# First FFN group freed by halves, weight tiles per phase, squares summed on VectorE

## The chip, the cores and the metric
The kernel runs as one program on one core of a Trainium2 chip. The metric is the device time of one launch in microseconds. Three runs of the kernel before took 2505.52, 2515.11 and 2516.34 us. The profile is one further execution of 2504.3 us.

## The reference
A stack of four layers on x of 512 tokens by 1024 features, in float32. Each layer is a mixer and a SwiGLU feed-forward network (FFN), both behind an RMSNorm and both added to x.

```
def rmsnorm(x, w):
    y = xf * lax.rsqrt(jnp.mean(xf * xf, axis=-1, keepdims=True) + EPS)
    return (y * w.astype(jnp.float32)).astype(x.dtype)
def swiglu(h, w_in, w_out):
    gu = h @ w_in
    gate, up = gu[..., :D_FF], gu[..., D_FF:]
    return (jax.nn.silu(gate) * up) @ w_out
...
    for i in range(DEPTH):                       # layers 0 and 1
        hn = rmsnorm(x, norm_mix_w[i])
        x = x + mlstm_mixer(hn, ...)             # or window_attn_mixer
        x = x + swiglu(rmsnorm(x, norm_ffn_w[i]), ffn_w_in[i], ffn_w_out[i])
    return rmsnorm(x, norm_final_w)              # then layers 2 and 3 and a last norm
```

D_FF is 2816. The mixers are, in order: mLSTM in both directions, attention in a window, a parallel layer (sparse attention with an indexer beside Mamba2), and a gated short convolution. The norm that ends layer 1 and the norm that opens layer 2 follow each other directly; the kernel does both in one pass, called the double norm here.

## The kernel before
x is kept transposed, as eight tiles xT[0..7] of 128 features by 512 tokens. Every float32 product is made of three fp32r matmuls: each operand is split into a part hi (rounded to fp32r) and a rest lo, and hi·hi, hi·lo and lo·hi are added in one PSUM bank (mm3, L206 to L208). For an activation the parts are xh and xl, for a weight whi and wlo.

Weights come in blocks of 512 KB into wraw (five buffers, SyncE's queue). ScalarE makes whi by a copy (L170), VectorE makes wlo by a subtraction (L165; in the parallel mixer GpSimd does most of them). Both have four buffers of 4 KB per partition, in one pool wp that lives for the whole program. TensorE's last matmul with a buffer frees it.

The norm (L255) needs the sum of squares of each token over all eight tiles. ScalarE squares a tile into sq (one buffer), GpSimd adds it to ssum (L271). Then TensorE sums ssum over the partitions (col_sums, L239), VectorE computes 1/sqrt in 128x4 steps (rsqrt_cols, L229 to L234), TensorE spreads the result over all partitions by four transposes (bcast_rows, L245), and ScalarE copies it to rb (L246). The matmuls don't wait for rb: they use x times the norm's weight, and the result is multiplied by rb.

An FFN works on groups of 256 hidden features. The first group (first(), L475) is done plainly while the norm finishes: 8 k-tiles for each of two gate and two up blocks, with banks "s", "o", "s", "o". Bank "o" is a single one in the FFN, so the second up block comes later, when the first has been read. The gate half goes through VectorE (times rb) and Silu on ScalarE. Every further group is done by seven products in place of eight (a Strassen scheme over two halves of k and two of the tokens): product() with 24 matmuls of 128x256 (L421 to L423), whose activation operands are parts of x (B11, B21, B22) or their combinations T1 to T4, made by combine() (L371 to L377: S, fu, thi, tlo), and whose weight operands are weights or sums of them (S, L400 on GpSimd, L405 on VectorE). ahead() keeps three products' weights in preparation. After the groups of a part, out_part multiplies by the down weights, and add_row adds the result to xT (L493, L494).

The order of the instructions on each engine is set by a scheduler, from the code's dependencies and its own costs, and is fixed when the program is built. TensorE, VectorE, ScalarE and GpSimd work in that order; a wait holds up all that stands behind it on its engine.

Of the kernel before, what the change touches and what calls it, by code (L numbers as in the profile page):

```python
# [16 lines left out]
P = 128  # L17
# [40 lines left out]
def tile_net(ctx: ExitStack, tc: tile.TileContext, d, out, layers=(0, 1, 2, 3)):  # L58
# [12 lines left out]
    wp = ctx.enter_context(tc.tile_pool(name="wp", bufs=4))  # L71
# [20 lines left out]
    hidden = [None, None]  # L92

# [10 lines left out]
    WB = 4  # L104
# [79 lines left out]
    def load_a(w, k0, nk, c0, n):  # L184

        res = [[] for _ in range(0, n, P)]
        for k in range(0, nk, 4):
            m = min(4, nk - k)
            raw = load_raw(w, k0 + k, c0)
            hi, lo = split(raw, m, n)  # L190
            for b in range(0, n, P):
                res[b // P] += [(hi[:, i, b:b + P], lo[:, i, b:b + P]) for i in range(m)]
        return res

    def load_b(w, k0, nk, c0, n):
# [3 lines left out]
        for k in range(0, nk, mk):  # L199
            raw = load_raw(w, k0 + k, c0)  # L200
            hi, lo = split(raw, mk, n)
            res += [(hi[:, i, :], lo[:, i, :]) for i in range(mk)]
# [33 lines left out]
    def col_sums(ssum):  # L236
        ps = bank("t")
# [4 lines left out]
    def bcast_rows(rc, rb):  # L242
        ps = bank("t")
# [11 lines left out]
    def norm(wname, pre=None):  # L255
# [27 lines left out]
        for i, ssum in enumerate(sums):  # L283
            v = scr("nv", (P, NCH))
            V.tensor_scalar(v, col_sums(ssum), 1.0 / D, None if i else EPS, op0=ALU.mult,
                            **({} if i else dict(op1=ALU.add)))
            if i:
                V.tensor_tensor(v, v, rcs[0], op=ALU.mult)
                V.tensor_tensor(v, v, rcs[0], op=ALU.mult)
                V.tensor_scalar(v, v, EPS, None, op0=ALU.add)  # L290
            r = scr("nrc", (P, NCH), bufs=3)
            rsqrt_cols(r, v, NCH)
            rcs.append(r)
        if pre:
            V.tensor_tensor(rcs[1], rcs[1], rcs[0], op=ALU.mult)
            xs.rb1 = bcast_rows(rcs[0], row_tile())
        xs.rc = rcs[-1]
        xs.rb = bcast_rows(xs.rc, row_tile())
        return xs

    def group_a(xs, blocks, banks):
# [39 lines left out]
    def ffn(L, last=False, aside=None):  # L341
        wi, wd = f"in{L}", f"down{L}"
        xs = norm(f"ffn{L}")
        parts = [(0, 3), (3, 6), (6, 9), (9, 11)] if last else [(0, 4), (4, 8), (8, 11)]
        hid = {}
        rb2 = bass.AP(tensor=xs.rb.tensor, offset=xs.rb.offset, ap=[xs.rb.ap[0], [0, 2], [1, S]])
        HS = slice(0, S // 2), slice(S // 2, S)

        def gate(g):
            V.tensor_tensor(g, g, rb2, op=ALU.mult)  # L350
# [61 lines left out]
        def product(jj, s, ps, start):  # L412
            hi, lo = live.pop((jj, "w", s))
            x = quad(STEPS[s])
            for j in range(2):
                o = ps[:, HS[j]]
                for i in range(4):
                    c = slice(j * P, (j + 1) * P)
                    w = hi[:, i, c], lo[:, i, c]
# [179 lines left out]
    def mlstm():  # L599
# [12 lines left out]
        for k in (0, 4):  # L612
            hi = wp.tile([P, 4, P], F32R, tag="whi", name="ghi", bufs=WB)
# [1114 lines left out]
```

## Time and profile before

| | |
|---|---|
| runs | 2505.52, 2515.11, 2516.34 us |
| profiled execution | 2504.3 us, span 2502.2 us, mean granted clock 0.979 |
| TensorE (PE) busy | 2391.4 us, 96% |
| VectorE (DVE) busy | 1865.7 us, 75% |
| ScalarE (ACT) busy | 1139.0 us, 46% |
| GpSimd (POOL) busy | 526.8 us, 21% |
| squares added on GpSimd (L271) | 56 instructions, 92.5 us |
| where the phases lie | FFN of layer 0 opens near 271 us, that of layer 1 near 848, the double norm lies near 1223, the FFN of layer 2 opens near 1598, the short-conv mixer near 1940, its FFN near 2140 |

The span is the time from the first to the last instruction of the profile. The matmuls are pipelined, so a single one is shown longer than its share of the time; the distance from one start to the next says more. In the chain of waits that ended last TensorE has 83%, VectorE 9%, ScalarE 3%. The granted clock is a share of TensorE's full rate of 2.4 GHz; its other level is 1.2 GHz, shown as 0.50.

### The profile page before, as it was taken

What the parts mean: (1) busy time and instruction counts of PE and PEld (TensorE: products, weight loads), DVE (VectorE), ACT (ScalarE), POOL (GpSimd) and SP (SyncE); (2) the same over time, 40 slices, a digit from 0 to 9 for tenths busy, and PEclk for the clock granted to TensorE, in tenths of its full rate; (3) what the DMA queues carried; (4) which work ended last, traced back from release to release, by engine and by line L of the source; (5) the groups of instructions that cost most, each with busy time, mean ns of one, the idle gap of its engine ahead of it and who ended that gap; (6) DMA issues with size and microseconds to landing.
All of it is one profiled execution on the core that took longest, in us unless ns stands there. A gap on an engine that the chain in (4) does not pass through costs nothing.

```text
span 2502.2 us, 35838 instructions
## 1 busy us (share of the span) xinstructions
PE 2391.4 (96%) x14196; PEld 2087.2 (83%) x14196; DVE 1865.7 (75%) x2664; ACT 1139.0 (46%) x1739; POOL 526.8 (21%) x350
## 2 busy tenths in 40 slices
PE   8999899999899899999799988999999999999998
PEld 6887799998767799999567766798989777899997
DVE  5676887777776787777779968886867645868767
ACT  4444544444576553434444445453534323545334
POOL 3211201012362301011646235410000200200100
PEclk9999899999999899999899999999999999999999
DMA  4332232323311132323212133233323323223232
GB/s 146 119 102 60 67 123 85 118 81 115 97 47 34 59 118 85 119 85 99 76 61 63 47 110 93 61 102 92 117 92 103 99 84 95 85 92 122 83 110 76
DMA packets 73431, 226.58 MB, mean 91 GB/s; under 512 B 10336, under 2 KB 14576, under 8 KB 73264
## 3 DMA queue, kind: packets, MB, share of 16 engines
q1 hardware_dynamic: 68896, 220.00, 27.8%
q10 hardware_dynamic: 4320, 4.21, 0.6%
q8 instruction: 111, 1.82, 0.3%
q14 instruction: 56, 0.46, 0.1%
q0 software_dynamic: 48, 0.10, 0.0%
HBM read 219.45 MB, written 2.20 MB: 89 GB/s over the span
## 4 chain that ended last, share of the span: by engine, by line
PE 83%; DVE 9%; ACT 3%; DMA 2%; issue 2%; POOL 1%; ACTq 0%; SPq 0%; DVEq 0%; POOLq 0%
PE ps_g L206 6%; PE ps_g L207 6%; PE ps_g L208 6%; PE ps_g L423 5%; PE ps_g L421 5%; PE ps_g L422 5%; PE ps_s L206 3%; PE ps_s L207 3%; PE ps_s L208 3%; PE ps_t L423 3%; PE ps_t L422 3%; PE ps_t L421 3%; PE ps_t L206 3%; PE ps_t L207 3%; PE ps_t L208 3%
## 5 line engine op out<-in xcount | busy, mean ns | idle before, releaser
L170 ACT ACTIVATE whi<-wraw 128x1024 fp32r<-128x1024 f32 x358 | 372.9, 1044 | 544.3 <-PE ps_g L207 150.8
L165 DVE TENSOR_TENSOR wlo<-wraw,whi 128x1024 fp32r<-128x1024 f32 (+1 forms) x329 | 428.5, 1306 | 186.9 <-ACT whi L170 186.0
L400 POOL TENSOR_TENSOR S<-wraw 128x1024 f32<-128x1024 f32 x40 | 110.0, 2749 | 1012.9 <-DMA wraw<-in_in_dram 949.4
L170 ACT ACTIVATE whi<-S 128x1024 fp32r<-128x1024 f32 x160 | 169.5, 1060 | 244.5 <-PE ps_g L422 110.3
L206 PE MATMUL ps_g<-xh,whi 128*128 128x512 f32 (+1 forms) x632 | 258.2, 409 | 9.2 <-DVE ucv L1602 2.3
L165 DVE TENSOR_TENSOR wlo<-S,whi 128x1024 fp32r<-128x1024 f32 x160 | 210.9, 1319 | 64.4 <-ACT whi L170 64.2
L207 PE MATMUL ps_g<-xl,whi 128*128 128x512 f32 (+1 forms) x632 | 254.3, 403 | 0.2 <-DVE xl L279 0.2
L208 PE MATMUL ps_g<-xh,wlo 128*128 128x512 f32 (+1 forms) x632 | 253.7, 402 | 0.0
L423 PE MATMUL ps_g<-thi,wlo 128*128 128x256 f32 x640 | 181.4, 283 | 0.3 <-DVE wlo L165 0.3
L422 PE MATMUL ps_g<-tlo,whi 128*128 128x256 f32 x640 | 181.3, 283 | 0.0
L421 PE MATMUL ps_g<-thi,whi 128*128 128x256 f32 x640 | 181.3, 283 | 0.0
L206 PEld LDWEIGHTS ps_g<-xh,whi 128*128 128x128 f32 (+1 forms) x632 | 120.9, 191 | 39.5 <-issue 5.3
L208 PEld LDWEIGHTS ps_g<-xh,wlo 128*128 128x128 f32 (+1 forms) x632 | 121.2, 192 | 27.9 <-issue 2.6
L207 PEld LDWEIGHTS ps_g<-xl,whi 128*128 128x128 f32 (+1 forms) x632 | 121.2, 192 | 26.1 <-issue 2.0
L271 POOL TENSOR_TENSOR ssum<-ssum,sq 128x512 f32<-128x512 f32 x56 | 92.5, 1651 | 236.8 <-ACT sq L270 236.8
L423 PEld LDWEIGHTS ps_g<-thi,wlo 128*128 128x128 f32 x640 | 122.9, 192 | 0.5 <-DVE wlo L165 0.5
L421 PEld LDWEIGHTS ps_g<-thi,whi 128*128 128x128 f32 x640 | 123.0, 192 | 0.1
L422 PEld LDWEIGHTS ps_g<-tlo,whi 128*128 128x128 f32 x640 | 122.9, 192 | 0.1
L421 PE MATMUL ps_g<-xh,whi 128*128 128x256 f32 x320 | 94.1, 294 | 17.7 <-ACT whi L170 17.7
L207 PE MATMUL ps_s<-hlo,whi 128*128 128x512 f32 x264 | 102.9, 390 | 0.0
L208 PE MATMUL ps_s<-hhi,wlo 128*128 128x512 f32 x264 | 102.8, 389 | 0.0
L206 PE MATMUL ps_t<-hhi,whi 128*128 128x512 f32 x264 | 102.8, 389 | 0.0
(552 smaller groups left out, 7097.2 us busy)
## 6 DMA issues: line engine op xcount, KB each, us to landing
wraw<-in_in_dram SPq DMA_DIRECT2D x176, 512.0 KB, 3.6
wraw<-in_down_dram SPq DMA_DIRECT2D x82, 512.0 KB, 3.6
wraw<-in_par_in_dram SPq DMA_DIRECT2D x30, 512.0 KB, 3.5
wraw<-in_mlstm_in_dram SPq DMA_DIRECT2D x24, 512.0 KB, 3.8
wraw<-in_sc_in_dram SPq DMA_DIRECT2D x24, 512.0 KB, 3.5
wraw<-in_attn_in_dram SPq DMA_DIRECT2D x12, 512.0 KB, 4.1
wraw<-in_par_out_dram SPq DMA_DIRECT2D x12, 512.0 KB, 3.6
mb<-drs SPq DMA_DIRECT2D x16, 256.0 KB, 4.6
```

What stands on the lines that cost most here:

```text
L165: (V if e == "V" else G).tensor_tensor(lo, x, hi.bitcast(F32), op=ALU.subtract)
L170: A.activation(hi, raw, AF.Copy)
L206: T.matmul(o, lhsT=w[0], rhs=x[0], start=start, stop=False)
L207: T.matmul(o, lhsT=w[0], rhs=x[1], start=False, stop=False)
L208: T.matmul(o, lhsT=w[1], rhs=x[0], start=False, stop=stop)
L271: G.tensor_tensor(ssum, ssum, sq, op=ALU.add)
L400: G.tensor_tensor(live[jj, "S1"], live[jj, 2], live[jj, 3], op=ALU.add)
L421: T.matmul(o, lhsT=w[0], rhs=x[i][0], start=start and i == j == 0, stop=False, skip_group_check=True)
L422: T.matmul(o, lhsT=w[0], rhs=x[i][1], start=False, stop=False, skip_group_check=True)
L423: T.matmul(o, lhsT=w[1], rhs=x[i][0], start=False, stop=end, skip_group_check=True)
```

## The change
1. *Weight buffers per phase.* The pool wp goes. Each phase opens a pool of its own: in a mixer 8 buffers of 2 KB for whi and as many for wlo, in an FFN 4 of 4 KB. A tile of the new pool stands on memory of the phase before and waits for the last reader of just that memory (reuse_waits="tile"). split() cuts a block into pieces of the pool's width: in mixers load_a by blocks of 128 columns, load_b by two k-tiles, so whi and wlo are 128x512 there, and twice as many.
2. *The first FFN group.* Its weights are loaded as gate k 0 to 3, up k 0 to 3, gate k 4 to 7, up k 4 to 7, and k runs in its natural order (before: 0, 4, 1, 5, ..., with rows permuted on the host), so that a tile is used up halfway. The Strassen quadrants are k 0 to 3 and 4 to 7, and combine(i) pairs tiles i and i + 4.
3. *The FFN's norm inside the group.* col_sums and the rsqrt are written between k = 3 and k = 4, the broadcast at k = 6, on bank "s"; the group's banks are "t", "o", "t", "o".
4. *Squares' sums on VectorE* (7 additions per norm, 14 in the double norm, 56 in all). In the double norm both rsqrt chains are written first, then the two broadcasts.

The diff, cut to its core:

```
-    wp = ctx.enter_context(tc.tile_pool(name="wp", bufs=4))
...
+    def weight_tile(tag, name, nk, n):
+        pool, bufs, _ = weight_pool
+        return pool.tile([P, nk, n], F32R, tag=tag, name=name, bufs=bufs)
+
     def split(raw, nk, n):
-        hi = wp.tile([P, nk, n], F32R, tag="whi", name="whi", bufs=WB)
-        lo = wp.tile([P, nk, n], F32R, tag="wlo", name="wlo", bufs=WB)
-        A.activation(hi, raw, AF.Copy)
-        sub(lo, raw, hi)
-        return hi, lo
+        res = []
+        st = max(1, min(nk, weight_pool[2] // n))
+        for k in range(0, nk, st):
+            hi, lo = weight_tile("whi", "whi", st, n), weight_tile("wlo", "wlo", st, n)
+            A.activation(hi, raw[:, k:k + st, :], AF.Copy)
+            sub(lo, raw[:, k:k + st, :], hi)
+            res += [(hi[:, i, :], lo[:, i, :]) for i in range(st)]
+        return res
...
-                G.tensor_tensor(ssum, ssum, sq, op=ALU.add)
+                V.tensor_tensor(ssum, ssum, sq, op=ALU.add)
...
-    def group_a(xs, blocks, banks):
+    def group_a(xs, blocks, banks, between={}):
...
+            if k in between:
+                between[k]()
...
-        xs = norm(f"ffn{L}")
+        xs = norm(f"ffn{L}", tag="s", later=True)
...
         def first():
-            order = [0, 4, 1, 5, 2, 6, 3, 7]
-            bg = [[b[k] for k in order] for b in load_a(wi, 0, KT, 0, 256)]
-            bu = [[b[k] for k in order] for b in load_a(wi, 0, KT, DFF, 256)]
-            pss = group_a(xs, [bg[0], bu[0], bg[1], bu[1]], ["s", "o", "s", "o"])
+            ws = [], [], [], []
+            for k in (0, 4):
+                for n, c in enumerate((0, DFF)):
+                    for hi, lo in split(load_raw(wi, k, c), 4, 256):
+                        for i in range(2):
+                            ws[n + 2 * i].append([t[:, i * P:(i + 1) * P] for t in (hi, lo)])
+            pss = group_a(xs, ws, ["t", "o", "t", "o"], {4: xs.sums, 6: xs.rows})
...
+    TILE = dict(reuse_waits="tile")
...
+            with wpool(f"wm{L}", 8, 512), tc.tile_pool(name=f"hm{L}", bufs=8) as hidden[0], \
+                    tc.tile_pool(name=f"mix{L}", bufs=2) as phase[0]:
                 mixers[L]()
...
+        with wpool(f"wf{L}", 4, 1024), tc.tile_pool(name=f"tf{L}", bufs=4, **TILE) as hidden[1], \
+                tc.tile_pool(name=f"hf{L}", bufs=4, **TILE) as hidden[0], \
+                tc.tile_pool(name=f"ff{L}", bufs=2, **TILE) as phase[0]:
             ffn(L, last=last, aside=rope_tables if before_window else None)
```

How the order moves, at three places. ScalarE at the opening of layer 0's FFN, before (xT_116 is xT[7], xT_115 is xT[6]; thi are the combinations' hi parts):

```order
150 L270 ACTIVATE sq<-xT_113 128x512
151 L270 ACTIVATE sq<-xT_114 128x512
152 L222 ACTIVATE thi<-fu 128x1024
153 L270 ACTIVATE sq<-xT_115 128x512
154 L222 ACTIVATE thi<-fu 128x1024
155 L270 ACTIVATE sq<-xT_116 128x512
156 L170 ACTIVATE whi<-wraw 128x1024 x2
157 L170 ACTIVATE whi<-S 128x1024
```

The same place after (xT_113 is xT[7], xT_112 is xT[6]):

```order
153 L289 ACTIVATE xh<-xT_112,cols 128x512
154 L394 ACTIVATE S<-xT_112,cols 128x512
155 L176 ACTIVATE whi<-wraw 128x1024 x4
156 L281 ACTIVATE sq<-xT_110 128x512
157 L289 ACTIVATE xh<-xT_113,cols 128x512
158 L232 ACTIVATE thi<-fu 128x1024
159 L394 ACTIVATE S<-xT_109,cols 128x512
160 L394 ACTIVATE S<-xT_113,cols 128x512
161 L232 ACTIVATE thi<-fu 128x1024
162 L281 ACTIVATE sq<-xT_111 128x512
163 L176 ACTIVATE whi<-wraw 128x1024
164 L281 ACTIVATE sq<-xT_112 128x512
```

Before, the group's four whi stood far ahead of this piece, among the mixer's, and the first products' whi (row 156) behind the last square. After, the group's four whi stand together in row 155, behind xT[6], and the first product's whi (row 163) stands ahead of the last squares.

ScalarE from layer 0's FFN to the window mixer, before (xT_112 to xT_116 are xT[3] to xT[7]):

```order
301 L278 ACTIVATE xh<-xT_112,cols 128x512
302 L170 ACTIVATE whi<-wraw 128x1024 x2
303 L278 ACTIVATE xh<-xT_113,cols 128x512
304 L270 ACTIVATE sq<-xT_112 128x512
305 L278 ACTIVATE xh<-xT_114,cols 128x512
306 L270 ACTIVATE sq<-xT_113 128x512
307 L270 ACTIVATE sq<-xT_114 128x512
308 L170 ACTIVATE whi<-wraw 128x1024
309 L278 ACTIVATE xh<-xT_115,cols 128x512
310 L170 ACTIVATE whi<-wraw 128x1024
```

And after:

```order
315 L289 ACTIVATE xh<-xT_111,cols 128x512
316 L281 ACTIVATE sq<-xT_111 128x512
317 L289 ACTIVATE xh<-xT_112,cols 128x512
318 L281 ACTIVATE sq<-xT_112 128x512
319 L176 ACTIVATE whi<-wraw 128x512 x8
320 L289 ACTIVATE xh<-xT_113,cols 128x512
```

The mixer's first four whi, which stood among the last tiles of x, have become eight of half the size that stand together behind xT[6].

TensorE at the end of the double norm, before (nrc are the norm's factors; L1115 transposes the indexer's key weights):

```order
6633 L207 MATMUL ps_g<-xl,whi 128x512
6634 L208 MATMUL ps_g<-xh,wlo 128x512
6635 L245 MATMUL ps_t<-ident,nrc 128x128 x8
6636 L1115 MATMUL ps_t<-ident,ikw 128x8 x4
6637 L206 MATMUL ps_g<-xh,whi 128x512
```

After, with the two pieces of the order that hold the broadcasts:

```order
6610 L218 MATMUL ps_s<-xh,wlo 128x512
6611 L255 MATMUL ps_t<-ident,nrc 128x128 x4
6612 L216 MATMUL ps_g<-xh,whi 128x512
```

```order
6634 L217 MATMUL ps_g<-xl,whi 128x512
6635 L218 MATMUL ps_g<-xh,wlo 128x512
6636 L255 MATMUL ps_t<-ident,nrc 128x128 x4
6637 L1140 MATMUL ps_t<-ident,ikw 128x8 x4
6638 L216 MATMUL ps_g<-xh,whi 128x512
```

The eight transposes that stood together are two sets of four now, with the 24 matmuls of rows 6612 to 6635 between them.

## Rows read from the trace of the kernel before
**Rows 1.** Busy time and share of the span of each engine, from the page
```profile
PE 2391.4 (96%) x14196; PEld 2087.2 (83%) x14196; DVE 1865.7 (75%) x2664; ACT 1139.0 (46%) x1739; POOL 526.8 (21%) x350
```
**Rows 2.** Timeline of PE: start us, us, instruction [idle before <-what ended it]
```profile
279.60 0.58 PE L421 MATMUL ps_g<-xh,whi 128*128 128x256 f32 x1 [8.11 <-ACT whi L170]
...
856.16 0.58 PE L421 MATMUL ps_g<-xh,whi 128*128 128x256 f32 x1 [8.12 <-ACT whi L170]
...
1225.06 0.62 PE L245 MATMUL ps_t<-ident,nrc 128*128 128x128 f32 x4 [1.96 <-DVE nrc L234]
1235.14 1.09 PE L245 MATMUL ps_t<-ident,nrc 128*128 128x128 f32 x4 [9.46 <-DVE nrc L295]
1238.45 0.56 PE L1115 MATMUL ps_t<-ident,ikw 8*128 8x8 f32 x4 [2.22 <-DVE ikw L1111]
...
1381.62 0.30 PE L1393 MATMUL ps_o<-pth,N 128*128 128x128 f32 x1 [2.57 <-DVE cy L1410]
...
1616.03 1.87 PE L239 MATMUL ps_t<-ones,ssum 128*128 128x1 f32 x8 [2.52 <-POOL ssum L271]
...
1644.68 0.50 PE L206 MATMUL ps_o<-xh,whi 128*128 128x512 f32 x1 [1.53 <-DVE fu L487]
...
1968.36 1.11 PE L245 MATMUL ps_t<-ident,nrc 128*128 128x128 f32 x4 [2.43 <-DVE nrc L234]
1971.61 0.79 PE L206 MATMUL ps_g<-xh,whi 128*128 128x512 f32 x1 [2.14 <-DVE ct L1601]
...
2161.20 0.65 PE L245 MATMUL ps_t<-ident,nrc 128*128 128x128 f32 x4 [0.53 <-DVE nrc L234]
```
**Rows 3.** Windows of PE: stretch, us, busy (instructions), granted clock, DMA share, GB/s
```profile
279.60:290.00 10.40, 10.40 (x56) 0.60 0.16 52
856.20:866.00 9.80, 9.80 (x63) 0.74 0.18 55
1235.10:1246.00 10.90, 8.64 (x29) 0.61 0.01 2
1616.00:1628.00 12.00, 10.31 (x52) 0.59 0.15 45
1968.40:1980.00 11.60, 9.46 (x29) 0.61 0.01 1
1382.00:1390.00 8.00, 7.91 (x29) 0.79 0.01 2
1640.00:1648.00 8.00, 5.00 (x26) 1.00 0.26 68
1598.00:1646.00 48.00, 39.28 (x225) 0.89 0.19 58
```
**Rows 4.** Timeline of ACT ahead of the first FFN's first product
```profile
277.97 0.63 ACT L270 ACTIVATE sq<-xT 128x512 f32<-128x512 f32 x1 [3.47 <-POOL ssum L271]
278.50 1.99 ACT L170 ACTIVATE whi<-wraw 128x1024 fp32r<-128x1024 f32 x2
```
**Rows 5.** Timelines: what one matmul, split or addition takes; from the page, the squares
```profile
1218.18 0.39 PE L206 MATMUL ps_g<-xh,whi 128*128 128x512 f32 x1
...
1222.71 0.39 PE L208 MATMUL ps_g<-xh,wlo 128*128 128x512 f32 x1
...
1937.79 0.63 ACT L170 ACTIVATE whi<-wraw 128x512 fp32r<-128x512 f32 x1 [0.35 <-PE ps_t L207]
...
1619.72 1.22 DVE L165 TENSOR_TENSOR wlo<-wraw,whi 128x1024 fp32r<-128x1024 f32 x1
...
1947.97 0.68 DVE L493 TENSOR_TENSOR fg<-ps_s,rb 128x512 f32<-128x512 f32 x1
...
L271 POOL TENSOR_TENSOR ssum<-ssum,sq 128x512 f32<-128x512 f32 x56 | 92.5, 1651 | 236.8 <-ACT sq L270 236.8
```
**Rows 6.** Timelines of DVE and POOL in the double norm
```profile
1235.03 1.19 DVE L1363 TENSOR_SCALAR nrc<-nrc 128x4 f32<-128x4 f32 x1
...
1226.40 9.80 POOL L1414 TENSOR_TENSOR xT<-xT,rb 128x512 f32<-128x512 f32 x8 [3.41 <-ACT rb L246]
```

More of the change, by code (lines that the diff above doesn't have):

```diff
@@ L1 @@
-from contextlib import ExitStack
+from contextlib import ExitStack, contextmanager
 import numpy as np
@@ L189, in load_a @@
             raw = load_raw(w, k0 + k, c0)
-            hi, lo = split(raw, m, n)
+            if weight_pool[2] >= m * n:
+                w4 = split(raw, m, n)
+                for b in range(0, n, P):
+                    res[b // P] += [(hi[:, b:b + P], lo[:, b:b + P]) for hi, lo in w4]
+                continue
             for b in range(0, n, P):
-                res[b // P] += [(hi[:, i, b:b + P], lo[:, i, b:b + P]) for i in range(m)]
+                res[b // P] += split(raw[:, :, b:b + P], m, P)
         return res
@@ L200, in load_b @@
             raw = load_raw(w, k0 + k, c0)
-            hi, lo = split(raw, mk, n)
-            res += [(hi[:, i, :], lo[:, i, :]) for i in range(mk)]
+            res += split(raw, mk, n)
         return res
@@ L234, in rsqrt_cols, with col_sums @@
             V.scalar_tensor_tensor(y, z, 1.5, y, op0=ALU.add, op1=ALU.mult)
-    def col_sums(ssum):
-        ps = bank("t")
+    def col_sums(ssum, tag="t"):
+        ps = bank(tag)
         for c in range(NCH):
@@ L240, in col_sums, with bcast_rows @@
         return ps[:, 0:NCH]
-    def bcast_rows(rc, rb):
-        ps = bank("t")
+    def bcast_rows(rc, rb, tag="t"):
+        ps = bank(tag)
         for c in range(NCH):
@@ L253, in row_tile, with norm @@
         return sp.tile([P, S], F32, tag="rb", name="rb", bufs=2)
-    def norm(wname, pre=None):
+    def norm(wname, pre=None, tag="t", later=False):
         xs = XS()
@@ L282, in norm, with scales, rows @@
         rcs = []
[L283 to L298, printed above, removed]
+        def scales():
+            for i, ssum in enumerate(sums):
+                v = scr("nv", (P, NCH))
+                V.tensor_scalar(v, col_sums(ssum, tag), 1.0 / D, None if i else EPS, op0=ALU.mult,
+                                **({} if i else dict(op1=ALU.add)))
+                if i:
+                    V.tensor_tensor(v, v, rcs[0], op=ALU.mult)
+                    V.tensor_tensor(v, v, rcs[0], op=ALU.mult)
+                    V.tensor_scalar(v, v, EPS, None, op0=ALU.add)
+                r = scr("nrc", (P, NCH), bufs=3)
+                rsqrt_cols(r, v, NCH)
+                rcs.append(r)
+            if pre:
+                V.tensor_tensor(rcs[1], rcs[1], rcs[0], op=ALU.mult)
+            xs.rc = rcs[-1]
+        def rows():
+            xs.rb = bcast_rows(xs.rc, row_tile(), tag)
+            if pre:
+                xs.rb1 = bcast_rows(rcs[0], row_tile(), tag)
+        xs.sums, xs.rows = scales, rows
+        if not later:
+            scales()
+            rows()
         return xs
-    def group_a(xs, blocks, banks):
+    def group_a(xs, blocks, banks, between={}):
         n = len(xs.t)
@@ L418, in product @@
                     c = slice(j * P, (j + 1) * P)
-                    w = hi[:, i, c], lo[:, i, c]
+                    w = [t[:, c] for t in ws[i]]
                     end = i == 3
@@ L612, in mlstm @@
         for k in (0, 4):
-            hi = wp.tile([P, 4, P], F32R, tag="whi", name="ghi", bufs=WB)
-            lo = wp.tile([P, 4, P], F32R, tag="wlo", name="glo", bufs=WB)
+            hi = weight_tile("whi", "ghi", 4, P)
+            lo = weight_tile("wlo", "glo", 4, P)
             G.memset(hi.bitcast(F32), 0.0)
@@ L1081, in parallel @@
             G.memset(raw[:, :, 72:96], 0.0)
-            hi, lo = split(raw[:, :, 0:112], 4, 112)
-            sm += [(hi[:, i, :], lo[:, i, :]) for i in range(4)]
+            sm += split(raw[:, :, 0:112], 4, 112)
         lay = ExitStack()
@@ L1617, in tile_net, with wpool @@
     rope = ExitStack()
+    TILE = dict(reuse_waits="tile")
+    @contextmanager
+    def wpool(name, bufs, width):
+        with tc.tile_pool(name=name, bufs=bufs, **TILE) as pool:
+            weight_pool[:] = pool, bufs, width
+            yield
     for n, L in enumerate(layers):
@@ L1625, in tile_net @@
         if L == 2:
[L1626 removed]
+            with wpool(f"wm{L}", 8, 512), tc.tile_pool(name=f"hm{L}", bufs=8) as hidden[0]:
                 parallel(n > 0)
         else:
[L1629 removed]
+            with wpool(f"wm{L}", 8, 512), tc.tile_pool(name=f"hm{L}", bufs=8) as hidden[0], \
+                    tc.tile_pool(name=f"mix{L}", bufs=2) as phase[0]:
                 mixers[L]()
```

18 lines of the change are left out of this document (6 added, 12 removed).

## The prediction
> **What bounds the kernel now.** I read five views in this order. The busy shares come first: TensorE is busy 96% of the span [rows 1], so there are some 111 us in which it stands still, and only these, and the stretches in which its clock is low, can be won back. The second view is TensorE's timeline, cut to the instructions that come after an idle stretch of 2 us or so [rows 2]. The reader is to see where they lie: each of the first two FFNs opens with a hole of 8 us that ends when ScalarE delivers a weight tile (L170); the double norm ahead of the parallel mixer has three holes (1.96, 9.46 and 2.22 us); the third FFN has several small ones; the short-conv mixer has two (2.43 and 2.14 us); the fourth FFN has almost none (0.53 us). The third view gives the granted clock behind such holes [rows 3]. Behind the first hole TensorE works 10.40 us at a mean of 0.60, so it loses 0.40 x 10.40 = 4.2 us more; behind the second 0.26 x 9.80 = 2.5 us. Not every hole does that: behind 2.57 us the loss is 0.21 x 7.91 = 1.7 us, and in 1640 to 1648, where two holes of about 1.5 us lie, the clock stays at 1.00. The fourth view is ScalarE ahead of the first hole [rows 4]: it waits 3.47 us for GpSimd's addition of squares before the last square, and only then turns the weights. The matmuls had ended at 279.60 - 8.11 = 271.49, and since all four weight buffers were theirs, nothing could be prepared earlier. The fifth view are the unit costs [rows 5] and what GpSimd does to VectorE [rows 6].
>
> **What the places cost now**, idle plus clock: first FFN 8.11 + 4.2 = 12.3; second 8.12 + 2.5 = 10.6; third 48 - 39.28 = 8.7 idle in the whole opening stretch, plus 0.41 x 10.31 = 4.2, together 12.9; fourth 0.53 in rows 2, I take 0.8 with what is below my cut. Four FFNs: 36.6. Double norm 13.64 + 0.39 x 8.64 = 17.0. Short-conv start 4.57 + 0.39 x 9.46 = 8.3. (All [rows 2, 3].)
>
> **The change part by part.** T is the end of the last matmul before a phase. A 128x512 matmul comes every (1222.71 - 1218.18) / 20 = 0.227 us; one of 128x256 I take at half, 0.113 (an estimate); a Strassen product has 24 of them, 2.7 us. Two whi of 4 KB take 1.99 us [rows 4], so 1.0 each; one of 2 KB 0.63; wlo of 4 KB 1.22; an addition of 128x512 on VectorE 0.68 [rows 5].
>
> (1) FFN openings. The group's first tile (gate k 0 to 3) is now used up halfway, so the first product's tile is turned while the group still runs, and the hole of 8 us goes. Three things are late next.
> First, the weights of the group itself. The pool is new per phase, so its tiles stand on memory that the mixer still reads: in the order, ScalarE's four whi come after xh and S of xT[6], and the last of them waits for T. The first whi ends near T + 0.5 (first FFN) or T + 1.0 (second, which waits for T itself); VectorE adds xT[7] (T + 0.8) and two 128x256 pieces before wlo, which ends near T + 2.7; TensorE has six matmuls (1.4 us) to do meanwhile. Idle: 2.7 - 1.4, about 1.4 us with latencies; third FFN 1.05 (no pieces in the way), fourth 0.7 (its first whi is early). Before, this cost nothing.
> Second, the third product. Until the second half of the "up" blocks is done (they share the one bank "o" and come after the fourth product), two of four buffers stay with the group. The third product's whi therefore waits for the end of the second product: 1.1 us to the first matmul, then wlo 1.22 of which two matmuls cover 0.2. That is 2.1 us idle in the first and second FFN, 3.0 in the third, where a subtraction of 1.2 us and two smaller things stand ahead of that wlo on VectorE, 1.6 in the fourth, where the broadcast covers 0.5.
> Third, the row broadcast. It now stands behind the third product, and the fourth product needs the bank that the gate is read from. Behind the transposes queue ScalarE's whi (1.1 us after the product), rb (0.63), and VectorE's wlo (to 2.3) and the multiplication (0.68): 3.0 in all, less some 0.5 of the transposes (four take up to 0.62 [rows 2]), 2.55 us. The fourth FFN has its broadcast earlier and pays nothing here.
> The clock: pairs of about 1.5 us left it alone, 2.57 us cost 1.7 [rows 2, 3]; the third hole is of that size, so I take 1.7 for each of the first three FFNs, with 0 and 4.2 as ends.
> After: 1.4 + 2.1 + 2.55 + 1.7 = 7.8 twice; 1.05 + 3.0 + 2.55 + 1.7 = 8.3; 2.3. Together 26.2 against 36.6: **-10.4**. Ends: the second and third hole could be covered by nothing that the trace shows, so they could also be 1.5 us each longer (4 x 3 = +12), or vanish where ScalarE and VectorE run ahead (about -14).
>
> (2) Double norm. Before, the two broadcasts stand together, and the chain for the second runs while GpSimd scales xT for 9.80 us; each of VectorE's tiny 128x4 steps then takes 1.19 us [rows 6], whereas the whole chain of twelve in the short-conv norm costs TensorE 2.43 us [rows 2]. After, both chains are computed first, 24 matmuls (5.4 us) stand between the broadcasts, and GpSimd's scaling follows the second. What is left is the wait for ikw behind the second broadcast, 2.2 us as now [rows 2], plus 0.8 for clock: 17.0 - 3.0 = **-14.0**. Ends: weight halves on GpSimd still run beside the chain, so up to 5 us may come back; at best 17 - 2.2.
>
> (3) Short-conv start. 24 matmuls now stand between sums and broadcast, so the 2.43 us go; the wait for ct stays (2.14), alone and with no clock behind it: 8.3 - 2.2 = **-6.1**. Ends 0 and -8.
>
> (4) FFN to mixer, three times. Before, the first mixer weights were turned while the FFN still multiplied; now eight whi of 2 KB stand together and the first waits for the FFN's last matmuls, with VectorE's wlo behind an add and a square's sum: 0.55 + 0.1 + 0.5, near 1.2 us each: **+3.6**. Ends 1.5 and 9 (with clock).
>
> (5) Squares on VectorE: 56 additions of 0.68 = 38 us there [rows 5], none on TensorE's path: the column sums stand 15 matmuls into the first product, at T + 20, and I count the last addition at T + 14 to 16. Cover gone, they would cost up to these 38. In the bargain xl and the small steps meet GpSimd less. Nothing.
> (6) 2 KB tiles in mixers: 2 x 0.63 for 1.0 on ScalarE, 0.25 more per tile; ScalarE is busy 46% [rows 1]. Nothing, with 0 to +4, since the parallel mixer is crowded on VectorE. The start of the program is split finer: nothing, 0 to -3.
>
> Sum: -10.4 - 14.0 - 6.1 + 3.6 = -26.9. The profiled execution took 2504.3 us (span 2502.2 and 2.1 around it), so it would take 2477. The median of the runs shown, 2515.11, lies 10.8 above; the forecast in its terms is **2488 us**.
>
> **Rivals.** (a) *The clock takes it back* (other side). The new holes lie close together: 1.4, then 2.1 and 2.55 within 6 us. If at each FFN both places drop the clock as the 8 us hole does, that is 8.4 us instead of 1.7 (0 in the fourth): +28.5, hence 2516; with a drop at the three mixer starts too, 3 x 4.2 more, 2529. It decides from the second place on in all four FFNs. For it: the third FFN's opening ran at 0.59 for 12 us with holes of 2.5 and less. Against: 1640 to 1648 at 1.00 [rows 3].
> The Trainium skill, "TensorE: Matmul & The Clock Gate", section "A second HAM failure mode: psum-queue depth-cycling", says that short idle stretches between groups of matmuls, if they come often enough, make the clock swing between its two levels; by that rule this rival's 2516 would come, and of this trace 1616 to 1628 agrees with it and 1640 to 1648 does not.
> (b) *VectorE becomes the bound.* It is busy 75% [rows 1], and gets 38 us of sums. If half of that stands on the path, 2488 + 19 = 2507. For: in the third FFN's opening and in the norms little of its time is free. Against: the sums are needed late.
> The Trainium skill, "SBUF — State Buffer", section "Who interferes with whom", says that a VectorE instruction with two SBUF inputs and a GpSimd instruction that reads SBUF lock each other out; the moved additions are of that kind, and the 1.19 us steps beside GpSimd's 9.80 agree in direction [rows 6].
> (c) *Better*: the second and third hole hardly appear and the clock holds: 26.2 falls to about 12, 2474.
> (d) *The halves free nothing*: the group's last buffers gate the products as before; the FFNs stay at 36.6, 2488 + 10.4 = 2498.
>
> **How the numbers follow.** Forecast 0.50, (c) 0.18, (d) 0.08, (b) 0.12, (a) 0.12. Half a percent, about what a measurement here tells from no change, is 12.6 us: 2502.5 and 2527.7. Faster: 0.50 + 0.18 + 0.08 = 0.76; same: 0.10 of (b) and 0.05 of (a); slower: 0.07 of (a) and 0.02 of (b), 0.09. Range 2466 to 2512: below (c) by the ends of (2) and (4), above (b), short of (a).
>
> **What would show it.** Right: no hole of 8 us at the FFN starts; in each FFN opening one of about 1.4 that ends with VectorE's wlo, one near 2.1 ended by ScalarE's whi and VectorE's wlo two products later, and one near 2.5 ended by VectorE's reading of the gate; the double norm with a single hole near 2.2; holes near 1.2 at the mixer starts. Wrong: a clock near 0.6 behind these, sums that end later than the first product, VectorE's busy share over 85% in the openings, or a hole of several us in the parallel mixer that is not there now.

## The result and the profile after

The changed kernel took 2479.14 us (median of four runs, 2478.45 to 2483.95), the kernel before 2512.11 beside it (four runs, 2505.52 to 2516.34). The ratio is 0.9875, with a 95% interval of 0.9848 to 0.9903. The forecast of 2488 us was made against a median of 2515.11; in its own terms, 2477.4 over 2504.3, it is 0.9893 and lies inside. The total was right; most of where it came from was not, and that the errors nearly cancelled was luck. The profiled execution of after took 2479.76 us (span 2478.1). That of before (2504.3) lies 8 us below the median of its runs, so the two profiles show some 24.5 of the 33 us.

The page of after, which answers to [rows 1]: GpSimd lost its 56 additions, VectorE's total hardly rose, TensorE's busy time fell by 3 us.

```profile
PE 2388.4 (96%) x14196; PEld 2088.1 (84%) x14196; DVE 1866.2 (75%) x2826; ACT 1160.3 (47%) x1869; POOL 437.2 (18%) x318
```

TensorE's timeline of after, which answers to [rows 2] (start, us, instruction, idle before and what ended it): the first FFN's opening, a piece of the second's, the double norm, the short-conv start.

```profile
248.38 0.50 PE L216 MATMUL ps_t<-xh,whi 128*128 128x512 f32 x1 [0.86 <-ACT whi L176]
...
251.00 0.73 PE L218 MATMUL ps_t<-xh,wlo 128*128 128x512 f32 x2 [0.95 <-DVE wlo L164]
...
271.50 0.38 PE L446 MATMUL ps_s<-xh,wlo 128*128 128x256 f32 x1 [1.27 <-DVE wlo L164]
...
275.42 0.39 PE L444 MATMUL ps_g<-thi,whi 128*128 128x256 f32 x1 [1.03 <-ACT whi L176]
...
276.68 0.39 PE L446 MATMUL ps_g<-thi,wlo 128*128 128x256 f32 x1 [0.76 <-DVE wlo L164]
...
283.72 0.58 PE L444 MATMUL ps_t<-thi,whi 128*128 128x256 f32 x1 [3.71 <-DVE fg L510]
...
859.02 0.39 PE L446 MATMUL ps_g<-thi,wlo 128*128 128x256 f32 x1 [0.76 <-DVE wlo L164]
859.24 0.28 PE L444 MATMUL ps_g<-thi,whi 128*128 128x256 f32 x1
859.36 0.37 PE L445 MATMUL ps_g<-tlo,whi 128*128 128x256 f32 x1
859.53 0.41 PE L446 MATMUL ps_g<-thi,wlo 128*128 128x256 f32 x1
859.74 0.41 PE L444 MATMUL ps_g<-thi,whi 128*128 128x256 f32 x1
...
1225.56 0.65 PE L255 MATMUL ps_t<-ident,nrc 128*128 128x128 f32 x4 [1.92 <-DVE nrc L308]
...
1228.39 0.56 PE L1140 MATMUL ps_t<-ident,ikw 8*128 8x8 f32 x4 [2.18 <-DVE ikw L1136]
...
1957.41 0.50 PE L216 MATMUL ps_g<-xh,whi 128*128 128x512 f32 x1 [2.14 <-DVE ct L1626]
```

The hole of 8 us is gone; in its place stand six, together 8.58 us, so TensorE is idle no less than before. The last ends when VectorE has read the gate. In the second FFN, in the middle of a product, the distance between starts goes from 0.12 to 0.21 us at 859.53: the clock fell half a microsecond behind a hole of 0.76, ahead of the gate's hole. At the double norm the 9.46 of [rows 2] is gone.

Windows of TensorE in after, answering to [rows 3] (stretch, us, busy and instructions, granted clock, DMA share, GB/s); the last is the window mixer without its ends:

```profile
274.00:282.00 8.00, 4.23 (x32) 1.00 0.43 156
282.00:290.00 8.00, 6.28 (x28) 0.57 0.00 0
857.00:865.00 8.00, 5.32 (x28) 0.79 0.35 131
865.00:873.00 8.00, 6.72 (x34) 0.79 0.00 0
1600.00:1608.00 8.00, 3.65 (x25) 0.93 0.26 74
1608.00:1616.00 8.00, 5.85 (x27) 0.64 0.33 124
1616.00:1624.00 8.00, 8.00 (x41) 0.79 0.00 0
1228.00:1236.00 8.00, 7.61 (x23) 0.57 0.05 19
1957.00:1965.00 8.00, 7.59 (x26) 0.79 0.21 68
605.00:829.00 224.00, 209.76 (x969) 0.95 0.19 59
```

ScalarE at the first FFN, answering to [rows 4]. The group's weight tiles start right behind xh and S of xT[6]. The first product's whi (255.85) is made while the group runs, ahead of the last squares. These still wait for additions, now VectorE's (1.62 and 2.65 us), but no weight tile stands right behind them.

```profile
246.04 0.73 ACT L289 ACTIVATE xh<-xT,cols 128x512 fp32r<-128x512 f32 x1 [1.05 <-DVE xT L348]
246.67 0.71 ACT L394 ACTIVATE S<-xT,cols 128x512 f32<-128x512 f32 x1
247.28 2.94 ACT L176 ACTIVATE whi<-wraw 128x1024 fp32r<-128x1024 f32 x3
...
255.85 1.05 ACT L176 ACTIVATE whi<-wraw 128x1024 fp32r<-128x1024 f32 x1
258.52 0.63 ACT L281 ACTIVATE sq<-xT 128x512 f32<-128x512 f32 x1 [1.62 <-DVE ssum L282]
261.80 0.63 ACT L281 ACTIVATE sq<-xT 128x512 f32<-128x512 f32 x1 [2.65 <-DVE ssum L282]
```

**Time by phase**, in us, from the end of the last matmul of the phase before to that of its own, read off TensorE's timeline in one profile of each kernel. The variants below are in it, to be read with the experiments. "par" is the parallel mixer with the double norm, "FFNs" the sum of the four.

| kernel | mLSTM | FFN 0 | window | FFN 1 | par | FFN 2 | conv | FFN 3 | FFNs |
|---|---|---|---|---|---|---|---|---|---|
| before | 255.0 | 356.7 | 219.9 | 355.3 | 408.3 | 358.9 | 189.2 | 349.5 | 1420.4 |
| after | 247.4 | 357.1 | 225.2 | 356.3 | 389.5 | 360.0 | 181.3 | 351.7 | 1425.1 |
| before, sums on VectorE | 254.5 | 354.0 | 223.0 | 354.0 | 406.4 | 359.2 | 188.7 | 349.0 | 1416.1 |
| before, order of double norm | 255.2 | 358.8 | 222.9 | 355.9 | 405.6 | 361.2 | 188.2 | 349.5 | 1425.3 |
| before, both of these | 253.6 | 353.7 | 226.0 | 354.2 | 392.8 | 360.8 | 188.0 | 349.0 | 1417.7 |
| after, sums on GpSimd | 247.5 | 354.7 | 228.1 | 353.0 | 399.0 | 362.0 | 182.1 | 352.3 | 1422.0 |
| after, one pool | 254.7 | 353.8 | 222.2 | 356.0 | 387.5 | 360.7 | 188.4 | 348.3 | 1418.7 |
| after, no halves | 245.3 | 354.4 | 224.3 | 353.2 | 391.5 | 359.8 | 181.5 | 352.1 | 1419.4 |
| after, norm ahead | 245.5 | 349.0 | 223.8 | 350.5 | 404.4 | 357.0 | 179.9 | 349.6 | 1406.0 |
| after, other banks | 247.0 | 346.4 | 223.0 | 346.4 | 393.6 | 348.8 | 181.4 | 348.6 | 1390.2 |

So the FFNs, for which most of the change was written, gave nothing (+4.7 together). The gain is the parallel mixer (-18.8), the short-conv mixer (-7.9) and the mLSTM mixer (-7.6). A phase whose code two kernels have in common differs by up to some 4 us between their profiles where the order of the instructions is nearly the same, and by 15 in the parallel mixer of "after, norm ahead", which the scheduler ordered in another way (experiment 10). So differences of 4 us in the table carry nothing, and there is one profile of each kernel.

### The profile page after: what moved, and what is told of

The parts are those of the page before. It is cut to its first block, busy times and chain, and to the rows that moved or that the text cites. A ratio compares the mean times of both kernels' runs of the same rounds, so it can differ in the third digit from the quotient of the medians.

```text
span 2478.1 us, 36192 instructions
## 1 busy us (share of the span) xinstructions
PE 2388.4 (96%) x14196; PEld 2088.1 (84%) x14196; DVE 1866.2 (75%) x2826; ACT 1160.3 (47%) x1869; POOL 437.2 (18%) x318
## 4 chain that ended last, share of the span: by engine, by line
PE 82%; DVE 10%; DMA 2%; ACT 2%; issue 2%; POOL 1%; ACTq 0%; SPq 0%; DVEq 0%; POOLq 0%
PE ps_g L216 6%; PE ps_g L218 6%; PE ps_g L217 6%; PE ps_g L446 5%; PE ps_g L445 5%; PE ps_g L444 5%; PE ps_s L216 4%; PE ps_s L218 3%; PE ps_s L217 3%; PE ps_t L444 3%; PE ps_t L445 3%; PE ps_t L446 3%; PE ps_t L217 3%; PE ps_t L216 3%; PE ps_t L218 3%; DVE wlo L164 2%
## 5 line engine op out<-in xcount | busy, mean ns | idle before, releaser
L176 ACT ACTIVATE whi<-wraw 128x512 fp32r<-128x512 f32 (+1 forms) x488 | 394.7, 819 | 614.0 <-PE ps_g L217 195.8
L164 DVE TENSOR_TENSOR wlo<-wraw,whi 128x512 fp32r<-128x512 f32 (+1 forms) x428 | 441.1, 1040 | 173.2 <-ACT whi L176 164.3
L423 POOL TENSOR_TENSOR S<-wraw 128x1024 f32<-128x1024 f32 x40 | 117.0, 2924 | 1161.7 <-DMA wraw<-in_in_dram 995.1
L164 POOL TENSOR_TENSOR wlo<-wraw,whi 128x512 fp32r<-128x512 f32 (+1 forms) x60 | 79.6, 1336 | 142.0 <-ACT whi L176 96.2
L217 PE MATMUL ps_t<-hlo,whi 128*128 128x512 f32 x264 | 102.7, 389 | 0.0
```

The source lines that it names most:

```text
L164: (V if e == "V" else G).tensor_tensor(lo, x, hi.bitcast(F32), op=ALU.subtract)
L176: A.activation(hi, raw[:, k:k + st, :], AF.Copy)
L217: T.matmul(o, lhsT=w[0], rhs=x[1], start=False, stop=False)
L423: G.tensor_tensor(live[jj, "S1"], live[jj, 2], live[jj, 3], op=ALU.add)
```

## The experiments

Ratios are to the kernel before, run on the same chip, with 95% intervals.

**1. Squares added on VectorE, in the kernel before.**
```
-                G.tensor_tensor(ssum, ssum, sq, op=ALU.add)
+                V.tensor_tensor(ssum, ssum, sq, op=ALU.add)
```


> The kernel before, with the 56 additions of squares (L271) moved from GpSimd to VectorE and nothing else. Theory (the 8 us holes before came from ScalarE waiting for GpSimd's additions, not from weight tiles that were held too long): the first product's whi follows the end of the group by about 1 us, the holes at the first two FFN starts fall from 8.1 to about 2 us without loss of clock, the third FFN loses its 2.5 us hole; about 25 us faster than before, near 2487. Rival (the halves of the group free the tiles, the additions were beside the path): the holes stay near 8 us, at most 5 us faster, 2507 or more.

Measured 2500.3 us, 0.9969 (0.9957 to 0.9982), between the two. TensorE's timeline at the first FFN and the double norm:

```profile
271.69 0.38 PE L421 MATMUL ps_g<-xh,whi 128*128 128x256 f32 x1 [0.66 <-ACT whi L170]
...
1233.07 1.09 PE L245 MATMUL ps_t<-ident,nrc 128*128 128x128 f32 x4 [11.61 <-DVE nrc L295]
```

With the tiles held as before and only the additions moved, the 8.11 us fell to 0.66 here, and 1.91, 0.27 and later 1.47 and 0.99 came: FFN 0 is 2.7 us shorter, not 8. So most of the big hole was cover for smaller lateness. The big hole itself came from ScalarE. ScalarE's timeline here:

```profile
270.59 1.04 ACT L170 ACTIVATE whi<-wraw 128x1024 fp32r<-128x1024 f32 x1
...
272.49 0.61 ACT L270 ACTIVATE sq<-xT 128x512 f32<-128x512 f32 x1
```

and the addition that the last square waits for in [rows 4], from GpSimd's timeline of before:

```profile
273.29 4.64 POOL L271 TENSOR_TENSOR ssum<-ssum,sq 128x512 f32<-128x512 f32 x1 [4.05 <-ACT sq L270]
```

That addition took 4.64 us, against a mean of 1.65. With the additions on VectorE the last square starts at 272.49 in place of 277.97, 5.5 us earlier. And the scheduler's order moved with the edit: the first product's whi now stands ahead of that square and no longer behind it, so it starts at 270.59 in place of 278.50, 7.9 us earlier. What the order would give alone, no run shows.

**2. Squares back on GpSimd, in the changed kernel** (the same line the other way).

> The changed kernel with the 56 additions of squares back on GpSimd and nothing else. Theory (the sums are read only 15 matmuls into the first product, so who makes them matters little once first() and the pools are changed, but sq has one buffer and ScalarE waits for its reader): holes of 1 to 4 us come back where ScalarE waits for GpSimd ahead of a whi, 5 to 12 us slower than the changed kernel, 2484 to 2491. Rival (the move to VectorE is the main gain): 20 us or more slower, 2500.

Measured 2489.0 us, 0.9908 (0.9880 to 0.9937), some 8 us above after by the ratios, whose intervals overlap. Nearly all of it lies in the parallel mixer (399.0 against 389.5). The 8 us holes did not come back in the FFNs, though the additions are GpSimd's again: the first product's whi is made at 260.14 us, ahead of the squares that wait for GpSimd (1.31 and 3.00 us). Holes of 2.4 to 4.1 us came at five phases' starts.

**3. No halves: the changed kernel with k interleaved in the first group**, so that every tile is read to the end.
```
-        for k in range(n):
+        for i, k in enumerate((0, 4, 1, 5, 2, 6, 3, 7) if between else range(n)):
```


> The changed kernel, but the first group takes k in the order 0, 4, 1, 5, 2, 6, 3, 7, so that all four weight tiles are read to the end (norm inside, pools and sums as changed). Theory (halves only hide the first product's conversion): the first product starts 1 us late and waits 1.2 us for wlo, some 2 us more idle in each FFN, about 8 us slower than the changed kernel, near 2487. Rival (halves are what took the 8 us holes away): holes near 8 us again with the clock behind them, 25 to 35 us slower, near 2510.

Measured 2474.28 us, 0.9868 (0.9853 to 0.9882): not slower than after. The holes of the first opening are 0.86, 0.94, 2.45, 0.59 and 0.76, together 5.60. Neither expectation came. Freeing the tiles by halves is worth nothing that can be measured here.

**4. One pool of 4 KB buffers for the whole program, in the changed kernel.**
```
-        with tc.tile_pool(name=name, bufs=bufs, **TILE) as pool:
-            weight_pool[:] = pool, bufs, width
-            yield
+        weight_pool[:] = wp, 4, 1024
+        yield
```


> The changed kernel with one weight pool of 4 buffers of 4 KB for the whole program again (and so 4 KB tiles in the mixers). Theory (a new pool per phase makes the first weights wait for the last matmul of the phase before): the holes at the phase starts go (0.9 and 0.9, 0.9 and 0.9, 1.5 and 1.4 at three FFN starts; 0.5 to 1.8 at three mixer starts), about 10 us less, near 2469. Rival (the 2 KB tiles bring more inside the mixers than the starts cost): the holes of 0.8 us in the short-conv mixer and those at the program's start come back, 0 to 8 us slower, 2479 to 2487.

Measured 2484.71 us, 0.9914 (0.9896 to 0.9931). In the table the mLSTM and short-conv mixers go back to their times before (254.7 and 188.4), and the FFNs lose the cost of a fresh pool (1418.7). The short-conv start:

```profile
1949.13 0.65 PE L256 MATMUL ps_t<-ident,nrc 128*128 128x128 f32 x4 [2.43 <-DVE nrc L245]
1951.92 0.79 PE L217 MATMUL ps_g<-xh,whi 128*128 128x512 f32 x1 [2.14 <-DVE ct L1627]
```

Both holes of [rows 2] stand there to the hundredth, and five more of 0.78 to 0.88 us behind them (4.1 us) as in the kernel before. What shortened these mixers are the 2 KB tiles and not the pool per phase: in experiment 7, with one pool of 2 KB tiles, they take 246.3 and 179.9 us.

**5. Other banks for the first group, in the changed kernel.** Bank "s" has three buffers in an FFN, "t" and "g" two, "o" one.
```
-        xs = norm(f"ffn{L}", tag="s", later=True)
+        xs = norm(f"ffn{L}", tag="g", later=True)
...
-            pss = group_a(xs, ws, ["t", "o", "t", "o"], {4: xs.sums, 6: xs.rows})
+            pss = group_a(xs, ws, ["s", "o", "s", "t"], {4: xs.sums, 6: xs.rows})
```


> The changed kernel with other PSUM banks in the first group: gate blocks on s, s, up blocks on o and t, the norm's sums and broadcast on g. No bank that the next four products write is then held by the gate, and the second up block doesn't wait for the first to be read, so all four weight tiles are used up within the group. Theory (the holes at the third and fourth product come from the two tiles held by the up blocks and from the gate's bank): holes of 1.0, 0.8 and 2.5 to 3.7 us go in the first three FFNs, with the clock behind them; 15 to 20 us less than the changed kernel, near 2461. Rival (VectorE and ScalarE are simply behind in the opening, whichever bank it is): the holes move to other products, 0 to 5 us less, 2474 to 2479.

Measured 2446.58 us, 0.9759 (0.9745 to 0.9774): 29 us below after by the ratios, more than was expected. TensorE's windows over the first three openings:

```profile
247.00:290.00 43.00, 41.91 (x259) 1.00 0.30 98
816.00:860.00 44.00, 42.67 (x266) 1.00 0.29 96
1556.00:1600.00 44.00, 42.26 (x250) 0.96 0.31 96
```

About 1.1 to 1.7 us idle in each, the clock at 1.00, 1.00 and 0.96. All four blocks have a bank, so the group's 96 matmuls run before the first product where 72 did, and no product waits for the gate: the FFNs are 34.9 us shorter than in after.

**6. The same banks without halves** (the edits of 3 and 5 together).

> The kernel with the other banks (e8), but with k in the order 0, 4, 1, 5, 2, 6, 3, 7 in the first group, so that no weight tile is used up before the group ends. Theory (with the banks out of the way the halves do their work: they let two products' weights be turned inside the group): a hole of 1.0 plus 1.4 us at each FFN's first product and about 1 at the second, with no clock behind it; 8 to 14 us slower than e8, 2455 to 2460. Rival (the halves are worth nothing here either, as with the banks of the changed kernel): within 3 us of e8.

Measured 2445.67 us, 0.9742 (0.9718 to 0.9765), the same as 5. Halves are worth nothing here either. These two are the best versions run.

**7. The same banks, with one pool of eight 2 KB buffers.**
```
+        weight_pool[:] = wp, 8, 512
```


> The kernel with the other banks (e8) and, in place of a pool per phase, one pool of 8 buffers of 2 KB for the whole program, so that weights are split in pieces of 128x512 in the FFNs too. Theory (the starts of the phases wait because a new pool stands on memory that is still read): the nine holes of 0.2 to 1.5 us at six phase starts go, 7 to 8 us, against some 45 us more work on VectorE that is hidden; 4 to 8 us faster than e8, near 2440. Rival (the extra splits are not hidden in the FFN openings): holes ended by VectorE's wlo, 2447 to 2460.

Measured 2451.13 us, 0.9763 (0.9740 to 0.9786): inside 5's interval. The value lies in the rival's range, but none of the holes left in the FFN openings ends with wlo. The holes at the phases' starts go, yet the FFNs take 1390.5 us against 1390.2, and the window mixer 227.8 against 223.0.

**8. Only the order of the double norm, in the kernel before.**
```
-            xs.rb1 = bcast_rows(rcs[0], row_tile())
         xs.rc = rcs[-1]
         xs.rb = bcast_rows(xs.rc, row_tile())
+        if pre:
+            xs.rb1 = bcast_rows(rcs[0], row_tile())
```


> The kernel before with one edit: in the double norm the broadcast of the final factors is written ahead of that of the first norm's factors. Theory (the 9.5 us hole came from the order: the second chain ran beside GpSimd's scaling of xT, which hangs on the first broadcast): the hole of 9.46 us shrinks to 3 to 4 us and the clock behind it holds or nearly, 8 to 10 us faster than before, near 2498. Rival (the chain is slow beside whatever GpSimd does there, or the scheduler keeps both broadcasts together): less than 3 us faster.

Measured 2506.0 us, 0.9976 (0.9960 to 0.9992). TensorE's timeline there:

```profile
1230.98 0.62 PE L245 MATMUL ps_t<-ident,nrc 128*128 128x128 f32 x4 [2.00 <-DVE nrc L234]
1233.87 1.12 PE L245 MATMUL ps_t<-ident,nrc 128*128 128x128 f32 x4 [2.26 <-DVE nrc L295]
1237.20 0.56 PE L1116 MATMUL ps_t<-ident,ikw 8*128 8x8 f32 x4 [2.22 <-DVE ikw L1112]
```

The hole of 9.46 is 2.26 now, as the order was said to make it; from the phase's start to ikw's matmul it takes 44.4 us in place of 51.6. The time fell by less, some 6 us by the ratio where 8 to 10 were expected.

**9. The order and the sums on VectorE, in the kernel before** (the edits of 1 and 8).

> The kernel before with two edits only: squares added on VectorE, and both chains of the double norm ahead of the two broadcasts. Each alone measured 0.9969 and 0.9976 of the kernel before. Theory A (their gains are separate): 0.9945, about 2497 us at the median of before. Theory B (in the double norm each alone leaves what the other would have removed, a hole of 11.6 us with the sums alone, and the low clock behind three holes with the order alone, so that together they give what the change gives there): 0.990 to 0.992, 2484 to 2489, with one hole near 2.2 and the clock at 0.9 or more between.

Measured 2488.14 us, 0.9904 (0.9887 to 0.9920). Theory A's 0.9945 is out, B's range holds the value, but not its reason. TensorE's timeline:

```profile
1226.91 0.65 PE L245 MATMUL ps_t<-ident,nrc 128*128 128x128 f32 x4 [3.47 <-DVE nrc L295]
1229.79 0.56 PE L1116 MATMUL ps_t<-ident,ikw 8*128 8x8 f32 x4 [2.22 <-DVE ikw L1112]
```

There are two holes, not one. Up to ikw's matmul the two edits nearly add: -0.7 (sums), -7.2 (order), -9.2 us (both; after has -9.4). The surplus lies behind, in the rest of the parallel mixer. There TensorE has the same 1704 matmuls in each kernel:

| kernel | rest of the parallel mixer, us | idle | busy | granted clock |
|---|---|---|---|---|
| before | 356.7 | 22.6 | 334.1 | 0.97 |
| sums | 355.5 | 16.3 | 339.2 | 0.94 |
| order | 361.2 | 22.7 | 338.5 | 0.95 |
| both | 350.5 | 18.3 | 332.2 | 0.96 |
| after | 347.3 | 17.8 | 329.6 | 0.97 |

The idle time falls by 4 to 6 us with the sums and not with the order. The surplus is in the busy time of the same matmuls, and so for the most part in the clock: each edit alone has some 5 us more than before, both together 2 less. Yet 99% of TensorE's rows there stand in the same order in "before" and "order", and in "sums" and "both" (77% between "before" and "sums"). Whether the edits did this or one execution of a kernel differs so from the next isn't shown, with one profile of each; thirteen runs of the kernel before on one chip lie between 2504.9 and 2518.45 us. Shown is that these two small edits give 0.96 of the change's 1.25%.

**10. The FFN's norm ahead of the group again, in the changed kernel**, with the banks of the kernel before.
```
-        xs = norm(f"ffn{L}", tag="s", later=True)
+        xs = norm(f"ffn{L}")
...
-            pss = group_a(xs, ws, ["t", "o", "t", "o"], {4: xs.sums, 6: xs.rows})
+            pss = group_a(xs, ws, ["s", "o", "s", "o"])
```


> The changed kernel, but the FFN's norm stands ahead of the first group again (sums and broadcast in bank t, the group's gate blocks in bank s as before the change); halves, pools and sums on VectorE stay. Theory (the openings of the changed kernel are set by banks: gate blocks in t and up blocks in the one bank o hold the weight tiles of products 3 and 4): with the gate blocks back in s the cluster of holes becomes smaller, 2471 to 2478 us, 0.985 to 0.988 of the kernel before, and the holes that end with the gate (fg) go. Rival (the sums inside the group are what the change gains at the openings): without them the chain sums, root, broadcast stands ahead of the group on VectorE or behind it on TensorE, one hole of about 2 us more at each of four openings, 2486 to 2492, 0.991 to 0.994.

Measured 2472.84 us, 0.9848 (0.9833 to 0.9863), as the theory said. No hole ends with the gate in the first opening (0.86, 0.60, 1.21, 0.27), and the FFNs are 19 us shorter than in after; the parallel mixer took 15 us more in this profile (holes of 4.60, 4.92 and 5.08). Its code is that of after, but the scheduler ordered it in another way: 73% of TensorE's rows behind ikw stand in the order of after, against 99% in experiments 3, 5 and 6, where the mixer takes 391.5 to 395.1 us. So a part of what the change gained there may be a better order and not the change itself; how much is open.

## Why the prediction was right, and where it was wrong

**(1) FFN openings: wrong.** Forecast 36.6 to 26.2 us. Measured, idle is 8.58, 7.30, 9.87 and 2.13, and the clock costs, as one less the granted clock times the busy time in the windows above, 2.7, 2.5, 4.1 and 0: together 37.2. The sum erred by 11.0 us. The step that failed stands at its head: that the hole of 8 us is there because the group holds the tiles, and goes because a tile "is now used up halfway". [Rows 2] and [rows 4] speak against it: the tiles were free at 271.49 and the whi began at 278.50, so 7.0 of the 8.1 us were ScalarE's lateness, the wait of 3.47 us for GpSimd's addition at its end, which I read as a detail of the hole. Experiment 1 takes the hole away with the tiles held to the end, and 3 and 6 show that the halves add nothing to that. Not shown is whether the halves alone would have done it: experiment 2 has them, with the additions on GpSimd and the whi ahead of the late squares, and has no such hole either; no run has the changed kernel with neither.

Of the three late steps that were to follow, each appeared where it was put. The starts of the first three FFNs took 6.6 us (3.85 forecast), the third products 7.9 (7.2), the gates 8.3 (7.65). Not foreseen was a wait at the second product (1.27, 1.26, 0.48; 3.0 together). The clock took 9.3 in place of 5.1. I had seen that the fourth product needs the gate's bank, but took the banks as given; experiment 5 shows that they are nearly the whole price: with other banks the four openings have 3.9 us of idle and 1.7 of clock.

The gate's hole in the first FFN is 1.26 us longer than in the second (2.45). Timelines of after, VectorE first and then GpSimd, each at this gate, at the second FFN's (from 862 on) and at the double norm (from 1215 on), which answers to [rows 6]:

```profile
280.58 2.48 DVE L164 TENSOR_TENSOR wlo<-S,whi 128x1024 fp32r<-128x1024 f32 x1 [3.30 <-ACT whi L176]
282.99 1.27 DVE L510 TENSOR_TENSOR fg<-ps_t,rb 128x512 f32<-128x512 f32 x2
...
864.40 1.23 DVE L164 TENSOR_TENSOR wlo<-S,whi 128x1024 fp32r<-128x1024 f32 x1 [4.78 <-ACT whi L176]
...
1217.02 1.09 DVE L244 SCALAR_TENSOR_TENSOR nrc<-rs_z,nrc 128x4 f32<-128x4 f32 x1
...
1225.54 0.17 DVE L1388 TENSOR_SCALAR nrc<-nrc 128x4 f32<-128x4 f32 x1
```
```profile
279.63 2.35 POOL L423 TENSOR_TENSOR S<-wraw 128x1024 f32<-128x1024 f32 x1 [14.59 <-DMA wraw<-in_in_dram]
...
862.01 2.38 POOL L423 TENSOR_TENSOR S<-wraw 128x1024 f32<-128x1024 f32 x1 [14.62 <-DMA wraw<-in_in_dram]
...
1215.52 7.58 POOL L164 TENSOR_TENSOR wlo<-wraw,whi 128x512 fp32r<-128x512 f32 x6 [8.47 <-PE ps_g L217]
```

The subtraction ahead of the gate takes 2.48 us where it takes 1.23 in the second FFN: it begins 0.95 us after GpSimd's addition of weights and ends 1.1 after it. In the second FFN that addition ends just before, at 864.39. The Trainium skill, "SBUF — State Buffer", section "Who interferes with whom", says that the pair of ports which VectorE shares with GpSimd is held by one of them alone at a time; these rows agree, down to the one running behind the other.

**(2) Double norm: right in kind, too large.** Forecast 17.0 to 3.0; measured 1.92 + 2.18 idle and 0.43 x 7.61 = 3.3 of clock, 7.4. The hole of 9.46 went by the order, as said (experiment 8). Two things were mis-sized: the first broadcast still waits 1.92 us for VectorE, whose 128x4 steps take 1.09 us while GpSimd subtracts weights (its row at 1215.52) and 0.17 when it doesn't, and the clock behind was put at 0.8 us. What made up for it was not in the sum: behind ikw the mixer is another 9.4 us shorter, and no run shows how much of that is the change's.

**(3) Short-conv start: right, but for 1.6 us of clock.** Forecast 8.3 to 2.2, measured 2.14 + 0.21 x 7.59 = 3.7. The 2.43 us went as said: 24 matmuls stand between the sums (1948.32) and the broadcast (1954.67). What let the scheduler put them there are the 2 KB tiles, which the prediction did not see: with 4 KB tiles no matmul stands between, and the hole stays (experiment 4); with 2 KB tiles in one pool they stand between again (experiment 7). The phase gave 7.9 us, since five small holes below my cut went as well.

**(4) Starts of the mixers: right.** +3.6 forecast; 0.73, 1.76 and 1.25 us of idle are 3.7. The window mixer took 5.3 us more, though its whole idle time is nearly the same (13.6 us before, 14.4 after) and its granted clock 0.95 against 0.96. A kernel whose window mixer is untouched (experiment 8) took 3.0 more too, so half of it may not be the change; why is open.

**(5) Squares on VectorE: forecast nothing, worth 8 us or more.** By the ratios 8 us alone in the kernel before, some 8 when taken back (there the intervals overlap), and together with the order 24. I asked only what 38 us more cost VectorE, and priced the 38 us well: no hole of TensorE's in after ends with an addition of squares. I didn't ask who waits for GpSimd's 92.5. The waiting itself did not get less: ScalarE's squares waited 32.8 us for additions in before and 30.5 in after. What counts is what stands behind a waiting square.

**(6) 2 KB tiles: forecast nothing to +4, gave some 14 us** in two mixers (7.3 and 7.1 by experiment 4), of which the FFNs' fresh pools may take some 6 back (1425.1 against 1418.7, no single FFN by more than 3.4).

**Rivals.** (a) was right that the openings' clock costs more than I took (9.3), and wrong in the total. (b) is out: VectorE stays at 75%. (c) is out: the second and third hole came in full. (d) comes nearest to the FFNs' part, they stayed as they were, though the first product no longer waits for the group. That the total still hit is luck, a sum of errors of opposite sign: +11.0 (openings), +4.4 (double norm), +4.1 each for the window mixer and the rest of the FFNs, against -11 (rest of the parallel mixer), -7.6 (mLSTM) and -3 (short conv). They leave 2 us between the -26.9 of the forecast and the -24.5 of the profiles.

## What to carry to other kernels

When a hole ends with a tile's preparation, look at what the preparing engine waited for just before, and try that single edit first: here one letter, the engine of an addition, did what the halves were meant to do. Then look at the order too, since the scheduler may move it along with any edit. When a group of matmuls is to free something early, count its PSUM banks with the buffers: a block without a bank of its own moves behind the next products and holds its weights with it. And price an addition to a busy engine against what the idle engine's lateness costs the work that stands behind those who wait for it, not against the busy engine's own free time alone.

## What was not expected of the hardware

The clock does not answer to a hole by its length alone. The same stretch of the parallel mixer, 120 us into the phase, in before and then in the kernel of experiment 8 (windows, and the largest hole in each from the timelines):

```profile
1306.90:1326.90 20.00, 18.11 (x89) 1.00 0.11 28
```
```profile
1319.39 0.33 PE L1393 MATMUL ps_o<-ptl,N 128*128 128x128 f32 x1 [1.48 <-DVE ptl L1385]
```
```profile
1312.80:1332.80 20.00, 18.37 (x81) 0.83 0.19 53
```
```profile
1318.62 0.47 PE L1394 MATMUL ps_o<-ptl,N 128*128 128x128 f32 x1 [1.48 <-DVE ptl L1386]
```

A hole of 1.48 us with the same releaser is followed by the full clock in one and by a mean of 0.83 in the other, which costs 0.17 x 18.37 = 3.1 us. TensorE's order there is nearly the same in both, and the holes ahead of it are too. So the price of such a hole is nothing or 3 us, and one profile cannot tell which a change will meet, or another run of the same kernel. This is the size by which like phases differ in the table, and it may be why two edits can give more or less than their sum. The prediction took 1640 to 1648 in [rows 3], two holes of 1.5 us at 1.00, as evidence that such pairs are harmless; 859.53 in after, where the clock fell behind 1.03 and 0.76, shows that they are not always.
